# ScalarE's stores on its own DMA queue, bonus and gate loads on GpSimd's, and two PSUM banks counted as taken in a hand-planned TensorE order

## The chip, the cores and the metric

The kernel runs on one core of one Trainium2 chip. TensorE (PE in the profile) does the matrix products, VectorE (DVE), ScalarE (ACT) and GpSimd (POOL) the elementwise work, and SyncE (SP) here only issues DMAs. The metric is device time in microseconds from launch to end. Three runs of the kernel before took 1831.24, 1832.81 and 1837.26 us, a median of 1832.81.

## The reference, cut to what matters

One layer over 1024 prompt tokens and 64 sample tokens (8 sequences of 8), model width 1024, all in float32:

```python
h = rmsnorm(x, norm_g)
q, k, v, ga, ps, gb, ma, mb = split(h @ w_in)
o = sliding-window attention(q, k, v)            # 16 heads, window 128, sinks, bias
ya = (o * silu(ga)) @ w_out_a
z = ps + (shift(ps) - ps) * mu                   # branch B: r, k, v and two low-rank inputs
decay = exp(-exp(-softplus(-(w0 + tanh(wl) @ w2)) - 0.5));  a = sigmoid(a0 + al @ a2)
kk = normalise(k * k_k);  k = k * (1 + (a - 1) * k_a)
for t: S = S * decay + (S @ -kk) (kk * a)^T + v k^T;  y = S @ r     # 16 heads, state 64 x 64
yb = (groupnorm(y) * lnx_g + lnx_b + sum(r * k * r_k) * v) * silu(gb) @ w_out_b
out = x + (sigmoid(ma) * ya + sigmoid(mb) * yb) @ w_o;  y = rmsnorm(out)
```

The results also hold the last 128 keys and values, the last shift rows and the final states.

## The kernel before

Tokens lie along the free dimension, channels on the 128 partitions. A dense product of one 128-column tile of the weights (`mm3`, tile `d`) is split in three passes of high and low parts, 24 matmuls for each of three chunks of 364, 364 and 360 tokens. It lands in one of two PSUM banks with the tag `d`.

The span has three stages. `start` norms the input. `rwkv` runs branch B, the dense products of the projections woven in. `attention` and `final` do branch A and the output.

In `rwkv` the prompt is cut in 16 steps s: four pairs of 128-channel groups by four quarters of 256 tokens (the last quarter has the 64 sample tokens too). A step goes through these streams, each a Python generator:

- `preps`: for each group of the pair, `quarter` loads keys and receptances (`zk`, `zr`), multiplies the low-rank inputs (`lo`, two results) and the squared norms (`kn`), and makes the arrays `Pp`, `kkn` and `KB`; `bonus` makes `sum(r k r_k) v` and stores it in `d_b`. ScalarE's first operation on the next keys, `kkn` (L648), waits for the load of `zk`.
- `fronts`: `scores` makes the key-query products `A` for both groups, 8 small matmuls into two banks; ScalarE (`ab`, L787) and VectorE (`am`, `X`, L793 and L794) copy them out; `invert` sends `ab` through DRAM (L831, L838), solves 15 short triangular steps on VectorE and sends the result back; `turn` transposes values and keys (`t_..v`, `t_..k`).
- `merges` and `chains`: the merge of the inverse (`q_..`) and the recurrence itself, four chunks with the products `c` and `y`.
- `samples` (`sample_chunk`, products `ss_a` to `ss_y`) and `posts` (`post`: group norm, bonus `bt` and gate `gt` loaded from DRAM, three products on GpSimd, store).
- last, the stream of dense products, which fills what the others leave free. `spill` is such a filler: it copies a result out (`copy`), or takes a sigmoid (`sig`) or a SiLU (`silu`), and stores it.

TensorE's order is written out by `drive`, a planner that walks the generators with a clock of its own (`clk`): a step that yields a delay and a bank's tag is ready when the delay is over and the bank's time in `free` has come. The first ready stream of the list above (chains, merges, fronts, preps, samples, posts, dense) goes on. After a step, each tag in `self.used` gets `free = clk + HOLD`, with `HOLD` 2.0. Only `ps` with one buffer puts a tag there. The tag `a` has two buffers, used by `A`, by the second result `lo` and by `kn`; it is not counted in `rwkv`. The first result `lo`, the transposes, `bo` and all of `ss_..` share the one bank `m`.

The other engines' instructions are put in order by a scheduler, from priorities and its own estimates. Each engine works through its order strictly, DMA issues included: an issue that waits holds up whatever stands behind it. In `rwkv` SP issues all loads and stores but those of `zz`, `gz`, `y`, the weights and half of `dinv`, which GpSimd issues. ScalarE issues none.

Of the kernel before, what the change touches and what calls it, by code (L numbers as in the profile page):

```python
# [11 lines left out]
AF = mybir.ActivationFunctionType  # L12
# [69 lines left out]
class Prog:  # L82
# [346 lines left out]
    def spill(self, idx, dst, kind="copy", scale=1.0):  # L429

        nc, ep = self.nc, self.ep

        def evac(c0, c1, ps):
            t = ep.tile([P, 364], F32, tag="zz", name=f"sp{idx}_{c0}", bufs=3)[:, :c1 - c0]
            if kind == "copy":
                nc.scalar.activation(t, ps, AF.Copy, scale=scale)
            else:
                x = ps
                if kind == "silu":
                    x = ep.tile([P, 369], F32, tag="pad", name=f"sx{idx}_{c0}", bufs=3)[:, :c1 - c0]  # L440
                    nc.scalar.activation(x, ps, AF.Copy)
                self.sig_neg(t, t, x, -1.0, 0.0)
                if kind == "silu":
                    nc.gpsimd.tensor_tensor(t, x, t, ALU.mult)
            for d, a, b in dst:
                lo, hi = max(a, c0), min(b, c1)
                if lo < hi:
                    nc.sync.dma_start(d[:, lo - a:hi - a], t[:, lo - c0:hi - c0])
        yield from self.dense(idx, self.hhi, self.hlo, evac)
# [204 lines left out]
    def quarter(self, g, q, gi, f, pre):  # L654
        nc, ep, cp = self.nc, self.ep, self.cp_
        nm = f"{g}_{q}"
        smp = q == 3
        n = 320 if smp else 256
# [5 lines left out]
        w2, zk, kkn, zr = pre  # L664
        yield f"pf{g}_{q}", WD + 4.0 * gi, "m"

        res = []
        pl = [self.ps("m", f"lo{nm}0"), self.ps("a", f"lo{nm}1", 2)]
        for j in range(2):
            t = E("e1", 2)  # L670
            ps = pl[j]
# [93 lines left out]
    def scores(self, g, q, gi, f):  # L765

        nc = self.nc
        nm = f"{g}_{q}"
        S, ab = f["q"][gi], f["ab"]
# [3 lines left out]
        for c0, cn, n0 in sets:  # L773
            mi, ms = (C_SI, C_SS) if c0 else (C_MI, C_MS)
            yield WA if c0 or gi else WR
            pvs = [self.ps("a", f"A{nm}{c0}{h}", 2).rearrange("p (c x) -> p c x", c=4) for h in range(2)]
            for c in range(cn):
                for h, hr in enumerate(halves):
                    self.mm(pvs[h][:, c, :], lhsT=KB[hr, c0 + c, :, :].rearrange("p a s -> p (a s)"),
                            rhs=S["smp"]["ra"][hr].rearrange("p a s -> p (a s)") if c0 else S["X"][hr, c, h::2, :], start=True, stop=True)  # L780
# [41 lines left out]
    def invert(self, nm, ab, n0, nn):  # L822


        nc, ep = self.nc, self.ep
        nb = 8 * nn
        np_ = 2 * nb
        s1 = self.dp.tile([4 * nn, 32, 32], F32, name=f"s1{nm}")
        s2 = self.dp.tile([2, 4, nn, 16, 16], F32, name=f"s2{nm}")
        for g in range(4):  # L830
            nc.sync.dma_start(s1[g * nn:g * nn + nn].rearrange("n j t -> j n t"), ab[32 * g:32 * g + 32, n0:n0 + nn, 32 * (g % 2):32 * (g % 2) + 32])  # L831
        Mf = ep.tile([P, 272], F32, tag="TM", name=f"TM{nm}", bufs=1)
# [7 lines left out]
        if n0:  # L840
# [3 lines left out]
            for s in range(7):  # L844
                w = 7 - s
# [5 lines left out]
        else:  # L851
            for s in range(15):
                w = 15 - s
# [127 lines left out]
    def sample_chunk(self, g, Z):  # L981
        nc, cp = self.nc, self.cp_
# [9 lines left out]
        nc.scalar.activation(sx[:, 0:2], ps, AF.Copy)  # L992
        nc.vector.tensor_copy(sx[:, 2], ps[:, 1])
        yield None, WH, "m"
# [24 lines left out]
        nc.gpsimd.tensor_tensor(sin, sin, Z["pc"].unsqueeze(2).to_broadcast([P, NB, HD]), ALU.mult)  # L1019
        nc.sync.dma_start(self.O["swkv"][g], sin)  # L1020

    def post(self, g, nm, t, w, y):
# [3 lines left out]
        rs = cp.tile([P, 320], F32, tag="gb", name=f"gn{nm}", bufs=2)[:, :w]  # L1026
        nc.sync.dma_start(bt, self.d_b[g][:, t:t + w])
        yield None, WP, "t"
# [12 lines left out]
        gt = cp.tile([P, 320], F32, tag="gb", name=f"gt{nm}", bufs=2)[:, :w]  # L1041
        nc.sync.dma_start(gt, self.d_g[g][:, t:t + w])
        nc.gpsimd.tensor_tensor(y, y, bt, ALU.add)
# [554 lines left out]
```

## Time and profile before

| | |
|---|---|
| median of three runs | 1832.81 us |
| the profiled execution | 1828.53 us |
| its span, first to last instruction | 1826.7 us |
| TensorE busy | 1686.3 us, 92% |
| VectorE, ScalarE, GpSimd busy | 1001.7, 899.5, 647.0 us |
| mean granted TensorE clock | 0.962 |

The page gives each engine's busy time, then the span in 40 slices, then the chain of work that ended last. A busy share says little by itself. What counts is where TensorE stands idle, what ended each such wait, and at what clock it went on.

### The profile page before, as it was taken

To read this page: it belongs to the slowest core of one execution; us is meant where nothing else is said; L and a number is where in the kernel's file an instruction comes from. 1 tells how busy PE (TensorE), PEld (TensorE's weight loads), DVE (VectorE), ACT (ScalarE), POOL (GpSimd) and SP (SyncE) were. 2 spreads that over 40 slices of the span, in tenths; PEclk is the share of its full clock that TensorE was granted. 3 is DMA by queue.
4 is the path that set the end of the run, shared out by engine and by line. 5 is a ranking of instruction groups with operands and counts; after the bars stand their busy time and mean duration, and the time that the engine had idled before them with its cause. 6 is when DMAs were issued, how large, how long until landed. Compare 5 with 4: busy or idle time off the path is not lost.

```text
span 1826.7 us, 36891 instructions
## 1 busy us (share of the span) xinstructions
PE 1686.3 (92%) x13792; PEld 1579.2 (86%) x13792; DVE 1001.7 (55%) x2840; ACT 899.5 (49%) x2257; POOL 647.0 (35%) x902
## 2 busy tenths in 40 slices
PE   6989889888988989889989899999999999999997
PEld 4889789787888878878988888999999999999997
DVE  5322655766766756675445655330566676544533
ACT  6445545544544555455546554535466655422332
POOL 5466445544655553445654233543100000000000
PEclk8899989998999999999999899999999899999999
DMA  4334433343433344432334342323521434464521
GB/s 159 108 123 138 106 100 98 104 105 96 120 90 108 97 122 113 109 93 89 102 119 124 112 105 72 90 86 112 175 67 57 155 109 149 140 204 136 197 80 61
DMA packets 233682, 206.86 MB, mean 113 GB/s; under 512 B 135904, under 2 KB 202608, under 8 KB 233472
## 3 DMA queue, kind: packets, MB, share of 16 engines
q1 hardware_dynamic: 214624, 149.33, 28.6%
q0 software_dynamic: 18880, 55.17, 9.4%
q8 instruction: 109, 1.79, 0.4%
q14 instruction: 69, 0.57, 0.1%
HBM read 140.42 MB, written 65.98 MB: 113 GB/s over the span
## 4 chain that ended last, share of the span: by engine, by line
PE 59%; DVE 16%; DMA 9%; issue 4%; POOL 4%; ACT 3%; SPq 2%; DVEq 0%; POOLq 0%; ACTq 0%
PE d L110 35%; PE wo L110 5%; PE c L110 3%; DVE TR L858 3%; DVE Tt L856 2%; PE s L110 2%; PE o L110 2%; DVE KB L715 2%; PE y L110 2%; PE pt L108 1%; PE A L110 1%; DMA TM<-s 1%; DMA s<-TR 1%; DMA wraw<-in_w 1%; SPq L838 1%
## 5 line engine op out<-in xcount | busy, mean ns | idle before, releaser
L110 PE MATMUL d<-hhi,whi 128*128 128x364 f32 (+1 forms) x1656 | 590.7, 357 | 14.8 <-ACT zz L391 4.3
L110 PE MATMUL d<-hlo,whi 128*128 128x364 f32 (+1 forms) x1656 | 559.7, 338 | 12.2 <-DVE hlo L339 8.3
L110 PEld LDWEIGHTS d<-hhi,whi 128*128 128x128 f32 x1656 | 323.2, 195 | 23.8 <-ACT zz L391 4.9
L110 PEld LDWEIGHTS d<-hlo,whi 128*128 128x128 f32 x1656 | 323.2, 195 | 23.7 <-DVE hlo L339 12.9
L110 PE MATMUL d<-hhi,wlo 128*128 128x364 f32 (+1 forms) x1656 | 339.5, 342 | 0.0
L110 PEld LDWEIGHTS d<-hhi,wlo 128*128 128x128 f32 x1656 | 283.9, 193 | 4.6 <-issue 1.6
L171 POOL TENSOR_TENSOR wlo<-wraw,whi 128x1024 fp32r<-128x1024 f32 x56 | 135.4, 2417 | 82.2 <-ACT whi L170 43.6
L170 ACT ACTIVATE whi<-wraw 128x1024 fp32r<-128x1024 f32 x90 | 94.9, 1054 | 75.7 <-PE d L110 55.9
L1433 POOL TENSOR_TENSOR xr<-xr,frs 128x256 f32<-128x256 f32 x2 | 1.8, 932 | 346.8 <-ACT frs L1430 346.8
L392 POOL TENSOR_TENSOR zz<-zz,pad 128x364 f32<-128x364 f32 (+1 forms) x75 | 72.7, 969 | 58.4 <-ACT zz L391 22.6
L948 POOL TENSOR_TENSOR sp<-vsu,pc 64x128 f32<-64x128 f32 x128 | 54.2, 424 | 97.7 <-DVE vsu L970 88.5
L390 ACT ACTIVATE pad<-d,prm 128x364 f32<-128x364 f32 (+1 forms) x75 | 40.7, 542 | 89.5 <-PE d L110 86.7
L856 DVE TENSOR_TENSOR Tt<-TM,TR 128x30 f32<-128x30 f32 (+10 forms) x240 | 58.6, 244 | 33.6 <-DMA TM<-s 28.3
L1172 ACT ACTIVATE sc<-sc,st 128x256 f32<-128x256 f32 (+1 forms) x128 | 61.8, 485 | 23.7 <-DVE st L1168 23.7
L1083 POOL TENSOR_TENSOR ylo<-ys,yhi 128x364 fp32r<-128x364 f32 (+1 forms) x6 | 6.5, 1084 | 180.8 <-PE ptc L108 153.7
L715 DVE TENSOR_TENSOR KB<-e,sg 64x256 f32<-64x256 f32 x128 | 65.6, 522 | 3.6 <-PE t_10k L108 1.5
L858 DVE TENSOR_TENSOR TR<-TR,Tt 128x30 f32<-128x30 f32 (+10 forms) x240 | 64.1, 267 | 5.9
L877 POOL DMA_DIRECT2D dinv<-s x80 | 42.5, 538 | 68.0 <-DMA s<-TR 68.0
L110 PE MATMUL d<-ol,whi 128*128 128x364 f32 (+1 forms) x192 | 64.2, 334 | 1.4 <-DVE ol L230 1.4
L110 PE MATMUL d<-oh,whi 128*128 128x364 f32 (+1 forms) x192 | 64.0, 334 | 1.4 <-ACT oh L229 1.4
L110 PE MATMUL d<-yhi,whi 128*128 128x364 f32 (+1 forms) x192 | 64.2, 334 | 0.0
L110 PE MATMUL d<-ylo,whi 128*128 128x364 f32 (+1 forms) x192 | 63.6, 331 | 0.0
(348 smaller groups left out, 3743.1 us busy)
## 6 DMA issues: line engine op xcount, KB each, us to landing
wraw<-in_w POOLq DMA_DIRECT2D x56, 512.0 KB, 4.0
wraw<-in_w SPq DMA_DIRECT2D x37, 512.0 KB
d_z<-zz POOLq DMA_DIRECT2D x48, 182.0 KB, 2.3
zv<-d_z SPq DMA_DIRECT2D x48, 128.0 KB
w<-d_c SPq DMA_DIRECT2D x24, 256.0 KB
d_m<-sp SPq DMA_DIRECT2D x32, 182.0 KB
stageo<-d_o SPq DMA_DIRECT2D x8, 544.0 KB
d_z<-zz POOLq DMA_DIRECT2D x24, 180.0 KB, 4.1
```

The lines of the kernel that those rows point to most:

```text
L108: self.nc.tensor.transpose(out, lhsT, rhs)
L110: self.nc.tensor.matmul(out, lhsT=lhsT, rhs=rhs, **kw)
L170: nc.scalar.activation(hi, raw, AF.Copy)
L171: (nc.vector if self.dve_lo else nc.gpsimd).tensor_tensor(lo, raw, hi.bitcast(F32), ALU.subtract)
L390: nc.scalar.activation(pad[:, 1:1 + m], ps[:, :m], AF.Copy, scale=mu)
L392: nc.gpsimd.tensor_tensor(z[:, :m], z[:, :m], pad[:, 0:m], ALU.add)
L715: nc.vector.tensor_tensor(KB[hr, :4, j, :], self.v64(t)[hr], self.d64(Pi, 1)[hr], ALU.mult)
L856: nc.vector.tensor_tensor(tv, M[:np_, s:s + 1, s + 1:16].to_broadcast([np_, cc, w]), R[:np_, 0:cc, s:s + 1].to_broadcast([np_, cc, w]), AL ...
L858: nc.vector.tensor_tensor(R[:np_, 0:cc, s + 1:16], R[:np_, 0:cc, s + 1:16], tv, ALU.add)
L877: (nc.gpsimd if a else nc.sync).dma_start(D[o:o + 16, n0:n0 + nn, 16 * a:16 * a + 16], s2[a, g].rearrange("n j t -> j n t"))
L948: nc.gpsimd.tensor_tensor(sp[h], vsu[h, c, :, h], pc[h, c].unsqueeze(2).to_broadcast([64, 2, HD]), ALU.mult)
L1172: nc.scalar.activation(sc[k], sc[k], AF.Exp, bias=st[:, 0, k:k + 1], accum_out=st[:, 1, k:k + 1])
```

## The change

Six edits:

1. `spill` stores its tiles from ScalarE's DMA queue, and those of kind `silu` from GpSimd's, in place of SP's.
2. `scores` puts `a` in `self.used`, so the planner holds the tag for 2.0 after the products `A`.
3. `quarter` yields once more after its wait for `m`, until `a` is free, and only then issues `lo` and `kn`.
4. `invert` issues its four stores of `ab` from ScalarE's queue (those of the samples stay on SP's).
5. `sample_chunk` makes the third part of `sx` on ScalarE, not VectorE, and stores the sample state from GpSimd's queue.
6. `post` loads `bt` and `gt` from GpSimd's queue.

```diff
@@ spill
-                    nc.sync.dma_start(d[:, lo - a:hi - a], t[:, lo - c0:hi - c0])
+                    (nc.gpsimd if kind == "silu" else nc.scalar).dma_start(d[:, lo - a:hi - a], t[:, lo - c0:hi - c0])
@@ quarter
         yield f"pf{g}_{q}", WD + 4.0 * gi, "m"
+        yield None, 0.0, "a"
@@ scores
             pvs = [self.ps("a", f"A{nm}{c0}{h}", 2).rearrange("p (c x) -> p c x", c=4) for h in range(2)]
+            self.used.add("a")
@@ invert
-            nc.sync.dma_start(s1[g * nn:g * nn + nn].rearrange("n j t -> j n t"), ab[32 * g:32 * g + 32, n0:n0 + nn, 32 * (g % 2):32 * (g % 2) + 32])
+            (nc.sync if n0 else nc.scalar).dma_start(s1[g * nn:g * nn + nn].rearrange("n j t -> j n t"), ab[32 * g:32 * g + 32, n0:n0 + nn, 32 * (g % 2):32 * (g % 2) + 32])
@@ sample_chunk
         nc.scalar.activation(sx[:, 0:2], ps, AF.Copy)
-        nc.vector.tensor_copy(sx[:, 2], ps[:, 1])
+        nc.scalar.activation(sx[:, 2], ps[:, 1], AF.Copy)
...
-        nc.sync.dma_start(self.O["swkv"][g], sin)
+        nc.gpsimd.dma_start(self.O["swkv"][g], sin)
@@ post
-        nc.sync.dma_start(bt, self.d_b[g][:, t:t + w])
+        nc.gpsimd.dma_start(bt, self.d_b[g][:, t:t + w])
...
-        nc.sync.dma_start(gt, self.d_g[g][:, t:t + w])
+        nc.gpsimd.dma_start(gt, self.d_g[g][:, t:t + w])
```

How the orders move is seen at one step of the recurrence, third quarter of the second pair. In the names below `A_100` and `A_101` are the two banks of key-query products, `lo_20` and `lo_21` the two low-rank products of the next quarter, `kn` its norms. TensorE before:

```order
L110 MATMUL A_100_5330<-X_739,KB_1_4852 128x128
L110 MATMUL A_101_5331<-X_739,KB_1_4852 128x128
L110 MATMUL lo_20_5347<-zl_2_5215,w_2_2_5217 128x256 x2
L110 MATMUL lo_21_5348<-zl_2_5215,w_2_2_5217 128x256 x2
L110 MATMUL kn_2_5359<-kkn_2_5221,bc 128x256
L110 MATMUL d_1_5172<-hhi_149,wlo_4823 128x364 x4
L110 MATMUL q_0c<-du_0_5328,ab_0_4537 32x32 x16
L110 MATMUL d_2_5419<-hhi_154,whi_4822 128x360
L110 MATMUL d_2_5419<-hlo_155,whi_4822 128x360
...
L110 MATMUL A_100_5424<-X_740,KB_1_4959 128x128
```

Behind the change, the same place on TensorE:

```order
L110 MATMUL A_100_5318<-X_739,KB_1_4837 128x128
L110 MATMUL A_101_5319<-X_739,KB_1_4837 128x128
L110 MATMUL ss_a<-ras_3_3635,sin_5159 64x2x8 x16
L110 MATMUL q_0c<-du_0_5316,ab_0_4525 32x32 x16
L110 MATMUL d_1_5272<-hhi_149,whi_4875 128x364
L110 MATMUL d_1_5272<-hlo_150,whi_4875 128x364
...
L110 MATMUL lo_20_5382<-zl_2_5198,w_2_2_5200 128x256 x2
L110 MATMUL lo_21_5383<-zl_2_5198,w_2_2_5200 128x256 x2
L110 MATMUL kn_2_5394<-kkn_2_5204,bc 128x256
L110 MATMUL A_100_5396<-X_740,KB_1_4955 128x128
```

Four dense matmuls, a round of the merge and the first sample product now stand between the first group's `A` and `lo`. The second group's `A`, which had four dense matmuls, a merge round and four more between `kn` and itself, now follows `kn` at once.

ScalarE at that place before (`e` is made from `lo`, `sg` from `e`):

```order
L648 ACTIVATE kkn_2_5365<-zk_2_5363,prm 128x256
L787 ACTIVATE ab_1_5198<-A_100_5330 64x256
L674 ACTIVATE e_2_2_5349<-lo_20_5347,prd 128x256
L675 ACTIVATE e_2_2_5349<-e_2_2_5349 128x256
L787 ACTIVATE ab_1_5198<-A_101_5331 64x256
...
L787 ACTIVATE ab_1_5198<-A_100_5424 64x256
L920 ACTIVATE ti<-q_0d 32x8x32 x2
L815 ACTIVATE vsu_1_5199<-t_10v 64x4x64 x2
L787 ACTIVATE ab_1_5198<-A_101_5425 64x256
```

And now (line numbers are one or two higher):

```order
L789 ACTIVATE ab_1_5181<-A_100_5318 64x256
L994 ACTIVATE sx_5352<-ss_a 128x128
L995 ACTIVATE sx_5352<-ss_a 128x64
L789 ACTIVATE ab_1_5181<-A_101_5319 64x256
L675 ACTIVATE e_2_2_5384<-lo_20_5382,prd 128x256
...
L789 ACTIVATE ab_1_5181<-A_100_5396 64x256
L833 DMA s_10_5413<-ab_1_5181 32x8x32
L922 ACTIVATE ti<-q_0d 32x8x32 x2
L833 DMA s_10_5413<-ab_1_5181 32x8x32
L817 ACTIVATE vsu_1_5182<-t_10v 64x4x64 x2
L789 ACTIVATE ab_1_5181<-A_101_5397 64x256
L833 DMA s_10_5413<-ab_1_5181 32x8x32 x2
```

Both copies of the first group's `A` now stand ahead of `e`, `kkn` of the next load has left this place, and four DMA issues stand among the copies of the second group's `A`.

GpSimd in a `post` of the first step, the second group, before:

```order
L1040 TENSOR_TENSOR ysb_01_2554<-ysb_01_2554,gn_0_3331 128x256
L1043 TENSOR_TENSOR ysb_01_2554<-ysb_01_2554,bt_0_3330 128x256
L948 TENSOR_TENSOR sp_13_3527<-vsu_1_2133,pc_1_2134 64x128 x2
L877 DMA dinv<-s_20_3208 16x8x16 x4
L1044 TENSOR_TENSOR ysb_01_2554<-ysb_01_2554,gt_0_3510 128x256
```

And now:

```order
L1042 TENSOR_TENSOR ysb_01_2554<-ysb_01_2554,gn_0_3323 128x256
L169 DMA wraw_3710<-in_w 128x1024
L1044 DMA gt_0_3502<-d_g_108 128x256
L1045 TENSOR_TENSOR ysb_01_2554<-ysb_01_2554,bt_0_3322 128x256
L1029 DMA bt_1_3662<-d_b_115 128x256
L424 TENSOR_TENSOR gz_0_3538<-gx_0_3539,gz_0_3538 128x364
L425 DMA d_g_110<-gz_0_3538 128x364
L1046 TENSOR_TENSOR ysb_01_2554<-ysb_01_2554,gt_0_3502 128x256
```

GpSimd now issues the gate's load itself, behind a load of weights, and waits for it a few instructions later.

TensorE's order is the same in both kernels up to the first `lo` that comes behind an `A`, and over its last 2206 rows, from within the attention stage to the end.

## Rows read from the trace of the kernel before

**Rows 1.** The page: busy time of engines (us, share of the span, instructions), and the granted clock of TensorE in 40 slices.

```profile
PE 1686.3 (92%) x13792; PEld 1579.2 (86%) x13792; DVE 1001.7 (55%) x2840; ACT 899.5 (49%) x2257; POOL 647.0 (35%) x902
PEclk8899989998999999999999899999999899999999
```

**Rows 2.** Busy time by stretch (`start` with the first projections, `rwkv`, and the rest): us, busy time of each engine with its instructions, then granted clock, DMA share and GB/s.

```profile
0.00:125.00 125.00, 97.00 (x456) 84.78 (x457) 42.59 (x77) 58.56 (x129) 66.25 (x92) 0.86 0.38 132
125.00:1250.00 1125.00, 1028.06 (x9559) 959.55 (x9558) 646.69 (x1879) 577.04 (x1486) 554.95 (x784) 0.97 0.38 104
1250.00:1827.00 577.00, 561.25 (x3781) 534.84 (x3779) 312.40 (x885) 263.89 (x644) 25.83 (x28) 0.98 0.40 128
```

**Rows 3.** What TensorE waited for over the span, by line: us in total, times, longest.

```profile
PE lo L110 <- ACT ab L787: 26.8, 13, 4.4
PE c L110 <- DVE vsu L960: 11.4, 12, 2.9
PE c L110 <- DVE xs L955: 9.9, 6, 3.9
PE ss_b L110 <- DVE sx L993: 8.6, 3, 3.8
...
PE ss_b L110 <- DVE sg L686: 2.8, 1, 2.8
...
PE A L110 <- ACT ab L787: 0.6, 1, 0.6
```

**Rows 4.** The timeline from 348.7 to 354 us, TensorE, ScalarE and VectorE at one place where `lo` follows `A`: start, us, engine, line, operation, count, and in brackets the idle time before it and what ended it.

```profile
348.71 0.33 PE L110 MATMUL d<-hhi,whi 128*128 128x364 f32 x1
348.88 0.33 PE L110 MATMUL d<-hlo,whi 128*128 128x364 f32 x1
...
349.82 1.16 PE L110 MATMUL A<-X,KB 64*128 64x128 f32 x16
...
352.45 0.43 DVE L794 TENSOR_TENSOR X<-A,rco 64x256 f32<-64x256 f32 x1
...
352.81 0.38 ACT L787 ACTIVATE ab<-A 64x256 f32<-64x256 f32 x1
...
353.24 0.79 PE L110 MATMUL lo<-zl,w 128*128 128x256 f32 x2 [1.83 <-ACT ab L787]
```

**Rows 5.** The timeline of ScalarE from 669 to 672 us and the TensorE row that waits for it.

```profile
669.50 0.51 ACT L648 ACTIVATE kkn<-zk,prm 128x256 f32<-128x256 f32 x1 [2.12 <-DMA zk<-d_z]
...
671.66 0.38 ACT L787 ACTIVATE ab<-A 64x256 f32<-64x256 f32 x1
...
672.09 0.80 PE L110 MATMUL lo<-zl,w 128*128 128x256 f32 x2 [4.20 <-ACT ab L787]
```

**Rows 6.** The timeline at one place where `A` comes after `kn`: ScalarE's and VectorE's copies out of the two banks between them.

```profile
302.77 0.70 PE L110 MATMUL kn<-kkn,bc 128*128 128x320 f32 x2
...
302.97 0.53 ACT L674 ACTIVATE e<-lo,prd 128x320 f32<-128x320 f32 x1
...
303.81 0.49 DVE L696 TENSOR_SCALAR kkn<-kn 128x320 f32<-128x320 f32 x1
```

**Rows 7.** The timeline at one sample step: the two parts of `sx`, and the product that reads them.

```profile
748.20 0.25 ACT L992 ACTIVATE sx<-ss_a 128x128 f32<-128x128 f32 x1
...
753.08 0.22 DVE L993 COPY sx<-ss_a 128x64 f32<-128x64 f32 x1
...
753.36 0.80 PE L110 MATMUL ss_b<-con,sx 128*128 128x128 f32 x2 [3.77 <-DVE sx L993]
```

**Rows 8.** Busy time in the seven stretches at half clock that come right behind a wait of `lo` (four) or of `ss_b` (three); columns as in the second group. The first of each kind, and the sum of all seven.

```profile
353.23:356.64 3.41, 3.40 (x71) 2.69 (x72) 2.52 (x5) 2.91 (x9) 1.18 (x2) 0.50 0.48 190
...
506.83:513.66 6.83, 6.20 (x24) 6.21 (x25) 1.00 (x5) 2.43 (x6) 4.73 (x9) 0.50 0.24 67
...
sum 34.13, PE 30.83 PEld 28.07 DVE 13.41 ACT 15.93 POOL 12.10; mean PE 4.40 PEld 4.01 DVE 1.92 ACT 2.27 POOL 1.73
```

**Rows 9.** Two lines' own views: how long SP takes for one DMA issue (ns, least, median, most).

```profile
L831 SPq DMA_DIRECT2D s<-ab x80: 302/418/1788, 190.6 to 1142.9; - x80
...
L448 SPq DMA_DIRECT2D d_m<-sp x48: 319/357/587, 555.7 to 1183.6; - x48
```

**Rows 10.** What SP's queue waited for over the span: us in total, times, longest.

```profile
SPq L448 <- ACT sp L222: 83.9, 23, 10.1
...
SPq L831 <- ACT ab L787: 74.9, 27, 12.9
...
SPq L646 <- DMA d_b<-zk: 35.0, 19, 3.8
```

**Rows 11.** Groups of GpSimd's instructions: count, busy us, mean ns, idle time before them and what ended it.

```profile
L1044 POOL TENSOR_TENSOR ysb<-ysb,gt 128x256 f32<-128x256 f32 (+1 forms) x32 | 26.4, 824 | 38.0 <-DMA gt<-d_g 37.5
...
L1045 POOL DMA_DIRECT2D d_y<-ysb x32 | 19.0, 594 | 12.8 <-POOL ysb L1044 6.5 <-issue 6.0 <-DVE TR L858 0.3
```

**Rows 12.** What ScalarE and VectorE waited for over the span: us in total, times, longest.

```profile
ACT kkn L648 <- DMA zk<-d_z: 72.8, 22, 10.8
...
DVE pad L387 <- POOL zz L392: 27.3, 5, 13.5
```

## The prediction

> **What bounds the kernel now.** I read the page's busy times first, then the busy times by stretch, then TensorE's waits, then the places themselves. TensorE is busy 92% of the span [rows 1]. In `rwkv`, from 125 to 1250 us, it is busy 1028 of 1125 us, so some 97 us stand idle there; the stretch behind it has 16 idle us in 577 [rows 2]. When the recurrence ends, dense work is still left, so time that TensorE loses in `rwkv` is lost for good. The change reaches `rwkv` almost alone, and the sum is made there.
>
> The waits name one culprit: `lo` on `ab`, 26.8 us in 13 waits [rows 3]. One place shows why [rows 4]. `A` ends at 350.98. Its banks are free only when VectorE's last `X` (352.88) and ScalarE's second `ab` (353.19) are done, 2.2 us later, but the order lets `lo`, which needs one of them, follow at once. TensorE stands 1.83 us. Another shows a long one [rows 5]: ScalarE sits 2.12 us on a load (`kkn`), the second `ab` ends at 672.04, and `lo` has waited 4.20 us. The `ss_b` waits are of the same kind: VectorE copies the third part of `sx` at 753.08, 4.6 us after ScalarE's part was done at 748.45, because it stands behind other work in its order [rows 7]. These two lines give 8.6 + 2.8 = 11.4 us [rows 3].
>
> Such a wait is paid twice. In the seven stretches at 0.50 behind waits of `lo` and `ss_b`, 34.13 us long, TensorE is busy 30.83 us at the lower of its two levels, 1.2 GHz, where 2.4 would have done the work in half: 15.4 us [rows 8].
>
> **The change part by part**, against the span of 1826.7 us (the whole execution took 1828.5, 4.3 under the median of the runs, and I add the same difference to the median).
>
> *The wait of `lo`.* In the planned order `lo` came at once, or within 0.9 us, behind `A` at 14 places. Counting the matmuls between at the trace's pitch (0.17 us for a dense one, 348.71 to 348.88 [rows 4]), there are now 1.2 to 2.6 us between. The second `lo`, the one that needs the bank, starts 0.3 us after the first, so a usual evacuation of 2.2 us leaves 0 to 0.7. The order of ScalarE helps: at most of these places both `ab` now stand ahead of the sigmoids of `lo`, and `kkn` has left several. The three waits over 3 us should keep about half. I leave 7 of 26.8: **-20** (ends -14, if only the 1.2 us of filling counts at each, and -27).
>
> *What follows it.* `lo` and `kn` take the same two banks, and these the planner still does not count. At most of the 14 places the second `A` now follows `kn` at once or after one short product, where some eight dense matmuls were. At one place of today `kn` ends at 303.47 and VectorE has its bank free at 304.30, 0.83 later; ScalarE's read of the second `lo` ends at 303.50 [rows 6]. So a new wait of about 0.5 us at each of 14 places: **+7** (2 to 14, the upper end if ScalarE is 1 us late, as it is behind one weight split or copy).
>
> *The bank `m`.* The new wait for `a` comes after the one for `m`, so another stream may take `m` in between, and does at five places: `ss_a` four times, a key transpose once, with 0 to 0.9 us between it and `lo`. ScalarE frees `m` with two copies of 0.25 each, behind one `ab` of 0.38 [rows 4, 7]; at the transpose two DMA issues stand ahead too. **+4** (1 to 9).
>
> *`sx` on ScalarE.* Its first part is read there anyway, 0.25 us; the second follows at once. **-9** of the 11.4 (0, if ScalarE is as late as VectorE was, to -11).
>
> *The clock.* Of 15.4 us I take 11 back, and give 3 to new waits long enough to bring the clock down: **-8** (0 to -15).
>
> *ScalarE's issues.* 64 stores of `ab` and 72 of filler results in `rwkv`. The trace shows no issue on ScalarE; the nearest rows are SP's, 0.36 to 0.42 us each [rows 9], so some 50 us on an engine that is busy 577 of 1125 [rows 2]. Two of them stand ahead of the copy of the value transpose at 16 places, 0.84 us before TensorE's key transpose needs the bank; the plan has 2 us there, which hides most. **+3** (0, if all is covered, to +13 if none is).
>
> *GpSimd's issues.* 64 loads, 8 state stores and 9 filler stores, 81 at 0.594 us, GpSimd's own price [rows 11], are 48 us on an engine busy 555 of 1125 [rows 2]. TensorE never waits for GpSimd directly there. What it can hold up is `zz`, for whose buffers VectorE waits [rows 12], and the state products. The wait for the gate's load exists already, 37.5 us [rows 11]; GpSimd now issues that load itself, right after the product that frees its buffer. **+3** (-2 to +40).
>
> *SP's queue.* It loses 222 issues and the waits ahead of them: it stood 83.9 us for filler results and 74.9 for `ab` [rows 10], with loads behind. ScalarE's 72.8 us of waiting for `zk` [rows 12] can shrink, but those loads wait for the bonus store that frees their buffer too (35.0 us [rows 10]). **-2** (0 to -6). The Trainium skill, page "DMA: Bandwidth & Descriptors", section "Issuing engines are not separate DMA queues", speaks against any gain here: issuing from several engines saves only the sequencer's time to start a DMA. By that this term is 0 and the time 2 us more; the rows above speak for waiting in line as a second thing that is saved.
>
> Sum: -20 + 7 + 4 - 9 - 8 + 3 + 3 - 2 = **-22 us**. 1832.8 - 22 = **1811 us**.
>
> **The rivals.**
>
> *All of it comes off.* ScalarE's new order takes the evacuations out of the way; -27 for `lo`, -11 for `ss_b`, -13 for the clock, new waits 2 + 1, and the issues +3 and +3 with -2: -44, 1789 us. For it: the long waits are ScalarE's order, and that order has changed. Against it: the second `A` right behind `kn`.
>
> *The wait only moves*, so that the change doesn't do what it says: `a` is counted for `A` alone, and the waits of `lo` turn up at the second `A` (+14) and at `m` (+9), with ScalarE's issues at +13 and new drops of the clock that use up what the old ones give back: -20 - 9 + 14 + 9 + 13 - 2 is -5, some 1828 to 1834 us, no change. For it: 14 places with next to nothing between `kn` and `A`. Against it: by the row of VectorE's copy that wait is a third of the old one [rows 6].
>
> *GpSimd becomes late*, slower. At each of the 32 posts it issues the gate's load and soon stops for it; with 0.594 for the issue and its landing behind, often with a load of weights just ahead in the same queue, `zz` and the state products come later, VectorE stands at L387 (already 27.3 us, once 13.5 [rows 12]), and the recurrence behind it. If 1.25 us of each post reach TensorE, that is +40 in place of +3: -22 + 37 = +15, 1848 us. It turns the result once 0.8 us of a post arrive (25 us over 32). For it: GpSimd works in strict order. Against it: half its time is free, and it waits for the same load today. The Trainium skill, page "DMA: Bandwidth & Descriptors", section "Latency and other measured facts", puts the first byte of a GpSimd DMA at about 1 us against 0.6 on the other queues; by that the 32 gate loads come 13 us later in all, an estimate from that page alone. No run here shows it.
>
> **How the numbers follow.** The sum 0.52 (its own range 1797 to 1826); all of it 0.12; only moved 0.19; GpSimd late 0.17. The range of 80% leaves out most of the second and the upper two thirds of the last: **1795 to 1840**. About 0.3% either way, 5.5 us, is what a measurement of this kernel can tell from no change. Under 1827.3 lie nearly all of the first two and a third of the third: **faster 0.68**, same 0.15, slower 0.17.
>
> **What would show it.** Right: `lo` on `ab` under 10 us, `ss_b` on `sx` under 3, the seven stretches at half clock mostly gone, `rwkv` idle near 75 us, and the tail from attention on unchanged. The steps of my additions: `A` waiting for `e` (L675) or `kkn` (L697) by 5 to 10 us, `lo` waiting for `sx` or `kbt` by about 4. Wrong: VectorE's waits for GpSimd's `zz` twice as long, with `c` on `vsu` and `xs` well over their 21 us; or the clock under 0.962 with the idle time moved, not gone.

## The result, and the profile after

| | before | after |
|---|---|---|
| median of four runs | 1832.03 us | 1853.03 us |
| ratio, 95% interval | | 1.0109 [1.0084, 1.0134] |
| profiled span | 1826.7 us | 1852.3 us |

The change makes the kernel 1.1% slower; the prediction had it 1.2% faster. The page of the changed kernel, its busy times and granted clock (against [rows 1]):

```profile
PE 1696.3 (92%) x13792; PEld 1591.6 (86%) x13792; DVE 1014.1 (55%) x2832; ACT 897.0 (48%) x2265; POOL 694.3 (37%) x983
PEclk8899999989899989999989999999999999999999
```

Busy time by stretch (against [rows 2]; us, then PE, PEld, DVE, ACT, POOL, clock, DMA share, GB/s):

```profile
125.00:1250.00 1125.00, 1010.33 (x9344) 944.67 (x9343) 654.76 (x1860) 559.14 (x1460) 579.98 (x838) 0.95 0.37 101
1250.00:1852.30 602.30, 587.64 (x3998) 561.00 (x3996) 316.95 (x896) 279.47 (x678) 48.28 (x55) 0.99 0.40 127
```

TensorE is busy 10 us longer with the same 13792 matmuls, at a mean granted clock of 0.956 against 0.962, and stands idle 15.6 us longer. GpSimd has 47 us more, for 81 DMA issues more. TensorE's waits over the span (against [rows 3]):

```profile
PE c L110 <- DVE vsu L962: 29.9, 16, 8.0
PE c L110 <- DVE xs L957: 20.0, 8, 6.3
PE bo L110 <- DVE vss L1007: 9.2, 3, 3.8
PE ss_a L110 <- DMA sin<-in_wkv: 8.9, 4, 3.9
...
PE ss_d L110 <- DVE ve L1015: 6.8, 2, 5.4
...
PE lo L110 <- ACT sx L995: 4.7, 1, 4.7
...
PE A L110 <- ACT e L675: 1.8, 3, 0.9
...
PE A L110 <- DVE kkn L697: 1.6, 3, 0.5
```

The wait of `lo` for `ab` is gone, and that of `ss_b` for `sx` too. `A` waits for `e` and `kkn` as foretold, but only 3.4 us. The recurrence's `c`, 21.3 us in [rows 3], now waits 49.9 us for VectorE. The stretches of `rwkv` at the lower clock, the first one and the sum of all 25 (against [rows 8], which held seven of 16):

```profile
224.13:230.96 6.83, 6.01 (x28) 5.38 (x29) 1.56 (x5) 4.05 (x12) 6.51 (x9) 0.50 0.35 83
...
sum 119.44, PE 103.51 PEld 97.57 DVE 60.23 ACT 38.69 POOL 46.70; mean PE 4.14 PEld 3.90 DVE 2.41 ACT 1.55 POOL 1.87
```

and the same sum over the 16 such stretches of the kernel before:

```profile
sum 78.49, PE 66.55 PEld 59.65 DVE 32.14 ACT 29.53 POOL 27.53; mean PE 4.16 PEld 3.73 DVE 2.01 ACT 1.85 POOL 1.72
```

TensorE works 103.5 us at 0.50 (1.2 GHz) in place of 66.6; at 2.4 GHz half would do, so 18.5 us more are lost in `rwkv`. Not all of that stays: behind 1250 us the clock is 0.99, where it was 0.98 before, and over the whole span the busy time grows by 10 us. These are also single executions, and the clock differs from one to the next: 0.956 to 0.963, mean 0.960, in four of the changed kernel; 0.954 to 0.973, mean 0.963, in 91 of the kernel before. So the size of the loss is uncertain. The gain of 8 that the prediction gave the clock shows nowhere.

GpSimd's loads (line groups; idle time before them at the end; against [rows 11]):

```profile
L1046 POOL TENSOR_TENSOR ysb<-ysb,gt 128x256 f32<-128x256 f32 (+1 forms) x32 | 26.6, 832 | 28.7 <-DMA gt<-d_g 28.4
...
L1044 POOL DMA_DIRECT2D gt<-d_g x32 | 18.6, 580 | 10.4 <-POOL ysb L1042 7.4 <-issue 3.0
L1029 POOL DMA_DIRECT2D bt<-d_b x32 | 17.8, 555 | 7.1 <-POOL ysb L1045 6.8 <-DMA d_b<-zk 0.3
```

### The profile page after: what moved, and what is told of

The parts are those of the page before. It is cut to its first block, busy times and chain, and to the rows that moved or that the text cites. A ratio compares the mean times of both kernels' runs of the same rounds, so it can differ in the third digit from the quotient of the medians.

```text
span 1852.3 us, 36813 instructions
## 1 busy us (share of the span) xinstructions
PE 1696.3 (92%) x13792; PEld 1591.6 (86%) x13792; DVE 1014.1 (55%) x2832; ACT 897.0 (48%) x2265; POOL 694.3 (37%) x983
## 3 DMA queue, kind: packets, MB, share of 16 engines
q0 software_dynamic: 23168, 67.86, 11.5%
## 4 chain that ended last, share of the span: by engine, by line
PE 57%; DVE 18%; DMA 8%; issue 5%; POOL 4%; ACT 3%; SPq 2%; DVEq 0%; ACTq 0%; POOLq 0%
PE d L110 35%; PE wo L110 5%; DVE Tt L858 3%; PE c L110 3%; DVE TR L860 3%; DVE KB L716 2%; PE s L110 2%; PE y L110 2%; PE o L110 2%; PE A L110 2%; PE pt L108 1%; DMA TM<-s 1%; SPq L840 1%; DMA wraw<-in_w 1%; POOL wlo L171 1%
## 5 line engine op out<-in xcount | busy, mean ns | idle before, releaser
L110 PE MATMUL d<-hhi,whi 128*128 128x364 f32 (+1 forms) x1656 | 588.6, 356 | 15.6 <-ACT zz L391 5.0
L110 PE MATMUL d<-hhi,wlo 128*128 128x364 f32 (+1 forms) x1656 | 346.9, 347 | 0.0
L110 PEld LDWEIGHTS d<-hhi,wlo 128*128 128x128 f32 x1656 | 289.2, 197 | 4.8 <-issue 0.7
L858 DVE TENSOR_TENSOR Tt<-TM,TR 128x30 f32<-128x30 f32 (+10 forms) x240 | 75.2, 313 | 16.5 <-DMA TM<-s 10.5
L110 PE MATMUL c<-vsu,kbt 128*128 128x128 f32 x256 | 43.3, 294 | 30.0 <-DVE vsu L962 29.9
L110 PEld LDWEIGHTS c<-vsu,kbt 128*128 128x128 f32 x256 | 38.0, 200 | 37.4 <-DVE vsu L962 35.2
```

The source lines that it names most:

```text
L110: self.nc.tensor.matmul(out, lhsT=lhsT, rhs=rhs, **kw)
L858: nc.vector.tensor_tensor(tv, M[:np_, s:s + 1, s + 1:16].to_broadcast([np_, cc, w]), R[:np_, 0:cc, s:s + 1].to_broadcast([np_, cc, w]), AL ...
```

## The experiments

Each of e1 to e18 was timed in five rounds beside the kernel before on one chip, but not all on the same chip, so ratios to the kernel before are compared, not times. `After` is the changed kernel, with the ratio of the four runs above; `before` is the one before.

| kernel | ratio | 95% |
|---|---|---|
| after | 1.0109 | 1.0084 to 1.0134 |
| e1: after, `bt` and `gt` back on SP | 1.0033 | 1.0013 to 1.0052 |
| e2: after, state store back on SP | 1.0117 | 1.0086 to 1.0148 |
| e3: before, banks alone (edits 2, 3) | 0.9997 | 0.9974 to 1.0019 |
| e4: after without the banks | 1.0075 | 1.0048 to 1.0102 |
| e5: e3, all uses counted | 0.9916 | 0.9885 to 0.9948 |
| e6: after, bias of `bt` made earlier | 1.0108 | 1.0080 to 1.0136 |
| e7: e3, the same | 1.0054 | 1.0030 to 1.0077 |
| e8: before, the same | 0.9994 | 0.9975 to 1.0014 |
| e9: after, all `dinv` loads on SP | 1.0174 | 1.0144 to 1.0204 |
| e10: after, `gt` back on SP | 1.0083 | 1.0052 to 1.0114 |
| e11: after, `bt` back on SP | 1.0131 | 1.0105 to 1.0156 |
| e12: after, all uses counted | 1.0024 | 1.0007 to 1.0040 |
| e13: e1 with 64 idle loads on GpSimd | 1.0186 | 1.0163 to 1.0210 |
| e14: before, `bt` and `gt` on GpSimd | 1.0117 | 1.0084 to 1.0150 |
| e15: before, stores on ScalarE | 1.0038 | 1.0018 to 1.0058 |
| e16: e5 with `sx` on ScalarE | 0.9923 | 0.9899 to 0.9948 |
| e17: e1 with 64 small stores on GpSimd | 1.0862 | 1.0828 to 1.0895 |
| e18: the same stores on SP | 1.0706 | 1.0672 to 1.0740 |

TensorE's order is the changed one in e1, e2, e3, e6, e7, e9 to e11, e13, e17 and e18, and that of before in e4, e8, e14 and e15, so orders and queues are told apart. Where the idle time lies, from the profiled runs: gaps of TensorE over 50 ns from 125 us to the recurrence's end, by the product that waited, and the time lost at the lower clock there (half of the work done at it), in us. Each row is one execution, and the last column is the least sure:

| | idle | lo | c | ss | A | rest | clock |
|---|---|---|---|---|---|---|---|
| before | 96.9 | 30.7 | 27.9 | 15.3 | 0.8 | 22.2 | 33.3 |
| after | 114.6 | 6.4 | 51.5 | 18.2 | 4.3 | 34.2 | 51.8 |
| e1 posts back | 102.9 | 6.6 | 43.1 | 16.3 | 4.3 | 32.6 | 36.6 |
| e3 banks alone | 95.9 | 7.1 | 41.1 | 14.7 | 7.5 | 25.5 | 38.9 |
| e4 no banks | 104.0 | 27.1 | 42.8 | 11.7 | 2.0 | 20.5 | 44.0 |
| e5 all counted | 84.9 | 2.8 | 30.6 | 29.4 | 4.5 | 17.6 | 33.1 |
| e14 posts alone | 108.4 | 31.4 | 32.5 | 17.7 | 0.8 | 26.0 | 44.8 |
| e15 stores alone | 103.7 | 23.6 | 38.2 | 19.3 | 1.3 | 21.3 | 44.6 |

**Which edit costs.** e1 and e2 undo one move of a queue, e3 does the banks alone, e4 leaves the banks out.

```diff
 e1  -        nc.gpsimd.dma_start(bt, ...)
     +        nc.sync.dma_start(bt, ...)          # gt likewise
 e2  -        nc.gpsimd.dma_start(self.O["swkv"][g], sin)
     +        nc.sync.dma_start(self.O["swkv"][g], sin)
 e3  +        yield None, 0.0, "a"                # on the kernel before
     +            self.used.add("a")
 e4  the two lines of e3 taken out of the changed kernel
```

> The changed kernel with the loads of bt and gt back on SP's queue, all else kept; TensorE's order is the same. Theory Loads (GpSimd issues the bonus and gate loads late, ScalarE stands for them, and the recurrence behind it): near the sum that I forecast, 1810 to 1828 us, ScalarE's wait for bt falls from 73 us to 40 or less, and the waits of c from 51 to under 35. Theory Order (the new order on TensorE leaves the recurrence too little time wherever the loads are issued): 1843 to 1855 us, c still waits 45 us or more. Theory State (the sample state's store on GpSimd holds up SP): 1845 to 1855.

> The changed kernel with the store of the sample state back on SP's queue, all else kept. Theory State: SP's wait at the load of the next state falls from 53 us to 10 or less, the waits of ss_a for that load (8.9 us) go, and the time falls to 1815 to 1835 us. Theories Loads and Order: only the 8.9 us and what they cost at half clock go, 1838 to 1852 us.

> The kernel before with the bank count alone (the tag a put in use by scores, and quarter's second yield): TensorE's order of the changed kernel, all DMAs and sx where they were. Theory Loads and theory State: the waits of lo fall from 27 us to under 10 and little comes in their place, 1812 to 1826 us. Theory Order: the waits of c rise as in the changed kernel, to 45 us or more, and the time is 1840 us or more.

> The changed kernel without the bank count: TensorE's order of the kernel before, with the new queues and sx on ScalarE. Theory Loads: the waits of lo are back and those of c are over 40 us, 1850 us or more. Theory State: much the same, 1845 or more, with SP's long wait at the load of the state. Theory Order: 1815 to 1832 us, the waits of c at 20 to 30 us as before.

The loads of `bt` and `gt` cost 1.0109 - 1.0033 = 0.76%, 14 us; the state store nothing that can be told (1.0117), so "State" falls. The banks, the heart of the forecast gain, bring nothing. What is left between e1 and e3 is 0.36%. No theory had the whole: e1 (1834 us) lies between the ranges of "Loads" and "Order", e4 (1840) between those of "Order" and "State", and e3 (1826) is far under the 1840 of "Order".

**Why the banks bring nothing.** e5 counts the bank `a` wherever it is used, and asks for `m` again once `a` is free; e16 adds the edit of `sx`.

```diff
 e5  (on e3)
             yield f"pf{g}_{q}", WD + 4.0 * gi, "m"
             yield None, 0.0, "a"
     +       yield None, 0.0, "m"
     ...
             pk = self.ps("a", f"kn{nm}", 2)
     +       self.used.add("a")
     ...
     -            yield WA if c0 or gi else WR
     +            yield None, WA if c0 or gi else WR, "a"
 e16 (on e5)
     -        nc.vector.tensor_copy(sx[:, 2], ps[:, 1])
     +        nc.scalar.activation(sx[:, 2], ps[:, 1], AF.Copy)
```

> The kernel before with the bank count made whole: quarter waits for m again after a, kn takes the tag a too, and scores waits for a before its products. TensorE's order differs from that of the banks-only kernel. Theory Ate-itself (the unguarded second A and the bank m ate the gain of the banks): the waits of A, lo and t (19.6 us in the banks-only kernel) fall under 8 us, c stays near 41, and the time falls by 8 to 15 us, to 0.992 to 0.996 of the kernel before. Theory Late-recurrence (TensorE only arrives earlier, and VectorE and ScalarE are not ready): those waits fall too, but c and q rise by as much, and the time is within 0.3% of the kernel before.

> The kernel with banks counted throughout (0.9916), with the third part of sx made on ScalarE as in the change. Its samples' products wait 29 us, of which some 19 stand behind VectorE's other work at ss_d, ss_y and ss_a. The prediction's step: ss_b no longer waits for VectorE's copy, worth up to 9 us where that wait exists; in this order it is small, so a theory 'No wait left' expects no change, ratio 0.990 to 0.993, some 1815 us; theory 'Still a gain' expects the 5 us of VectorE's time freed and the clock with it, ratio under 0.989, some 1809 us.

Dense matmuls that stand between the products of the two banks, counted in the traces:

| | A to lo: none between | kn to A: none between |
|---|---|---|
| before | 12 of 29 | 0 of 30 (least 4) |
| after (and e3) | 0 of 28 (least 4) | 13 of 29 |
| e5 | 0 of 21 (least 4) | 0 of 22 (least 8) |

The half count moves the bare place from `lo` to `A`. One such place after the change, TensorE, ScalarE and VectorE in the timeline (start, us, engine, line, operation, idle time before):

```profile
186.72 0.59 PE L110 MATMUL kn<-kkn,bc 128*128 128x256 f32 x2
...
187.35 0.42 DVE L697 TENSOR_SCALAR kkn<-kn 128x256 f32<-128x256 f32 x1 [1.65 <-PE kn L110]
187.35 0.84 ACT L675 ACTIVATE e<-lo,prd 128x256 f32<-128x256 f32 x2
...
188.25 0.94 PE L110 MATMUL A<-X,KB 64*128 64x128 f32 x12 [0.93 <-ACT e L675]
```

This costs little by itself (A 7.5 us in e3). But idle time in `rwkv` is 95.9 us in e3 against 96.9: what `lo` gives, `c` (+13.2), `A` (+6.7) and the merge and transposes take. With all uses counted, 12 us of idle go, `c` is back near 30, and the kernel is 0.8% faster than before. "Ate-itself" has the time, a little past its range, but not all of the way there: it had `c` stay near 41, and the waits of `A`, `lo` and the transposes fell from 19.6 to 11.4 us, not under 8, while the samples' products wait 29.4 us in place of 14.7. That the count was half done, and that the full one wins, is shown; which of its three lines wins is not told apart, and that `c` waits longer because dense work which had stood ahead of it now stands ahead of `lo` is argued only: with the stores alone, on the old order, `c` rises by 10 us too (e15). `sx` gains nothing here, as "No wait left" had it.

**What the loads on GpSimd cost by.** The first theory was ScalarE's stand for `bt`, 73.4 us in the change. e6 to e8 take ScalarE's operation on `bt` out of `post` and add the same bias ahead of the store of the bonus.

```diff
     -        nc.scalar.activation(bt, bt, AF.Identity, bias=self.par(Q_LB + g))
 bonus:
     +        nc.scalar.activation(zk[:, :n], zk[:, :n], AF.Identity, bias=self.par(Q_LB + g))
              nc.sync.dma_start(self.d_b[g][:, a0:a0 + n], zk[:, :n])
```

> The changed kernel, with the addition of the group norm's bias to bt moved from post (where ScalarE waits for the load of bt) to bonus, so that ScalarE has no instruction that waits for that load; GpSimd still issues it. TensorE's order is the same. Theory Loads (ScalarE standing for bt holds up gn, then VectorE's copy of ysb, then c): ScalarE's 73 us of waiting for bt go, VectorE's wait for gn falls from 67 us to under 40, c from 51 to under 40, and the ratio to the kernel before falls from 1.011 to 1.003 or less. Theory Issue (GpSimd's time for issues is what costs): c stays over 45 and the ratio at 1.008 to 1.012.

> The bank count alone, with the same move of the bias; loads on SP. ScalarE waits 65 us for bt in the banks-only kernel. Theory Loads: the gain of the banks shows once that wait is gone, 0.985 to 0.993 of the kernel before. Theory Late-recurrence (other causes): 0.996 to 1.002.

> Control: the kernel before with the move of the bias alone; ScalarE waits 40 us for bt there. Theory Loads: 0.993 to 0.999. Theory Late-recurrence: 0.998 to 1.003.

Nothing is won (1.0108 against 1.0109). That alone doesn't refute the theory, because ScalarE's new operation in `bonus` stands as long for VectorE's product. What speaks against it is e1: with 14 us won back, ScalarE stands for `bt` almost as long as in the change. The change, e1 and e6:

```profile
ACT bt L1035 <- DMA bt<-d_b: 73.4, 22, 6.7
...
ACT bt L1035 <- DMA bt<-d_b: 69.4, 21, 10.5
...
ACT zk L731 <- DVE zk L730: 72.7, 17, 7.5
```

On the banks alone the same move costs 0.57% (e7 against e3), which neither theory had and nothing here explains; on the kernel before it does nothing (e8).

TensorE's order being the same, the change and e1 can be laid side by side, matmul by matmul: by 1247 us the change is 24.7 us behind (16.1 at the end of the span), and some 21 of them arise in the seven stretches of 25 us that end at 338, 388, 489, 820, 971, 1046 and 1247. The one at 464 to 489, GpSimd, VectorE and TensorE:

```profile
462.50 0.58 POOL L1044 DMA_DIRECT2D gt<-d_g  x1 [2.98 <-issue]
...
464.15 0.55 POOL L1029 DMA_DIRECT2D bt<-d_b  x1 [0.31 <-DMA d_b<-zk]
...
464.72 2.12 POOL L879 DMA_DIRECT2D dinv<-s  x4
...
468.39 0.45 DVE L882 STREAM_TRANSPOSE dt<-dinv 128x256 f32<-128x256 f32 x1 [5.92 <-DMA dinv<-s]
468.56 2.33 POOL L171 TENSOR_TENSOR wlo<-wraw,whi 128x1024 fp32r<-128x1024 f32 x1
468.76 2.40 DVE L746 SCALAR_TENSOR_TENSOR X<-kkn,Pp 64x256 f32<-64x256 f32 x1
...
472.60 0.61 DVE L962 COPY vsu<-c 64x128 f32<-64x128 f32 x2
...
473.27 1.01 PE L110 MATMUL c<-vsu,kbt 128*128 128x128 f32 x3 [7.96 <-DVE vsu L962]
```

Behind the two loads stand GpSimd's four loads of the inverse's result; SP had issued its half by 461.0. VectorE stands 5.92 us for them, with the copy that the recurrence needs behind. Three runs vary this.

```diff
 e9  -   (nc.gpsimd if a else nc.sync).dma_start(D[o:o + 16, ...], s2[a, g]...)
     +   nc.sync.dma_start(D[o:o + 16, ...], s2[a, g]...)
 e10 -   nc.gpsimd.dma_start(gt, ...)
     +   nc.sync.dma_start(gt, ...)
 e11 -   nc.gpsimd.dma_start(bt, ...)
     +   nc.sync.dma_start(bt, ...)
```

> The changed kernel, with all loads of the inverse's result (dinv) issued from SP; half of them stood on GpSimd's queue in both kernels. Three theories of the 0.76% that the loads of bt and gt cost on GpSimd. Theory 'Behind': GpSimd stops at a load of gt or bt (for the bonus store or a buffer), and the dinv loads behind it go out late: at 466.8 against 461.0 on SP, and at 843.0 against 838.7, after which VectorE stands for dinv 5.92 and 3.1 us and the recurrence behind it; it expects 8 to 11 us less than the changed kernel, some 1842 us, ratio 1.005, and those two waits under 2 us. Theory 'Gate': what costs is that the product with the gate ends later, so that the buffer of the next post's group norm comes late and VectorE stands at the copy of the centred values (41.6 us against 30.8 with the loads on SP); it expects under 4 us here, some 1850 us, ratio 1.010. Theory 'Issue': what costs is GpSimd's time, 0.57 us an issue; 64 issues go from it here, as many as the loads were, so it expects most of the 14 us back, some 1840, and GpSimd's own products earlier everywhere.

> The changed kernel with the gate's loads (gt) back on SP and the bonus loads (bt) still on GpSimd. Theory 'Gate': nearly all of the 14 us come back, some 1837 us, ratio 1.004, VectorE's wait at the copy of the centred values back near 31 us. Theory 'Behind': half or less, since GpSimd still stops for the bonus store ahead of dinv, 3 to 7 us, some 1845 us. Theory 'Issue': half, 7 us, some 1844 us, and the next kernel gives the other half.

> The changed kernel with the bonus loads (bt) back on SP and the gate's loads (gt) still on GpSimd. Theory 'Gate': at most 3 us, some 1849 us, ratio 1.010, VectorE's wait at the copy of the centred values still near 40 us. Theory 'Behind': 4 to 8 us, since the stop for the bonus store ahead of dinv is gone, some 1845 us. Theory 'Issue': half, 7 us, some 1844 us.

In e9 that place is cured (`c` waits 3.54 us at 468.95), and VectorE's wait for `dinv` falls from 38.3 to 24.0 us, but the kernel is no faster (1.0174), with 80 issues more on SP and VectorE standing 12.7 us for a load (`TR`) that SP issues: "Behind" is true of the place and false of the sum. "Issue" falls short too, since it expected 1.005 here. e10 and e11 can't be told from the change. Against e1 the bonus loads alone cost 0.50% (e10) and the gate's loads alone 0.98% (e11), where both cost 0.76%: each move costs by itself, and the two don't add. "Gate" expected 1.004 of e10, "Behind" and "Issue" some 1.007 of e11, so none of the three has the whole.

e14 makes the same move on the kernel before, so that nothing else is in play.

> The kernel before, with the loads of bt and gt issued from GpSimd and nothing else changed. If this edit costs by itself what it costs inside the change, the ratio is 1.0076, some 1844 us. Theory 'Only together': the loads cost because the new order of TensorE has the recurrence waiting (41 us in place of 28 with the banks' edit alone), so that a late VectorE always shows; on the old order, whose idle time lies at lo, they cost under 0.3%, ratio under 1.003, some 1833 us.

It costs 1.17% alone. "Only together" falls. Its profiled execution shows no one waiter: idle rises by 11.5 us, spread over `c`, `bo`, `ss` and `lo`, and the clock takes another 11.5. The next three ask whether the issues themselves cost, or what they wait for.

```diff
 e13 (on e1)  in each post, behind each of the two loads
     +        nc.gpsimd.dma_start(cp.tile([P, 1], F32, tag="du", ..., bufs=8), self.I["par"][:, 0:1])
 e17 (on e1)  behind the product with rs and behind the sum with bt
     +        du = cp.tile([P, 1], F32, tag="du", ..., bufs=8)
     +        nc.gpsimd.tensor_copy(du, y[:, 0:1])
     +        nc.gpsimd.dma_start(self.dp.tile([P, 1], F32, ...), du)
 e18 as e17, but
     +        nc.sync.dma_start(self.dp.tile([P, 1], F32, ...), du)
```

> The changed kernel with the loads of bt and gt back on SP (1.0033 by itself), and two more loads in each post issued from GpSimd, at the same places: a column of parameters, 128 rows of one number, into a small tile that nothing reads. They wait for no other engine's work. Theory 'Issue': 64 issues at 0.57 us of GpSimd's time are the cost; the ratio is back near 1.010, some 1846 us. Theory 'Wait': what costs is that GpSimd stops in its order for the bonus store and the gate's buffer, and that the gate's load goes out only after GpSimd's own earlier product; then the ratio stays under 1.006, some 1835 us.

> The changed kernel with the loads of bt and gt back on SP (1.0033), and in each post two small stores more from GpSimd: a copy of one column of y into a small tile, behind the product with the group norm and behind the sum with the bonus, and a store of that tile to a scratch place in DRAM. They stand in GpSimd's order where the moved loads stood, and wait for GpSimd itself alone. Theory 'Issue': 64 issues at 0.55 us (and 64 small copies) on GpSimd, ahead of its products, are what costs: ratio 1.009 to 1.013, some 1848 us. Theory 'Wait': the loads cost because of what they wait for and because they go out late; these issues do neither: ratio under 1.006, some 1837 us. In between both have a share.

> The control: the same copies on GpSimd, but the 64 small stores issued from SP. What this kernel costs over 1.0033 is the copies, the transfers and SP's queue; only what the one before costs over this one is GpSimd's issuing. Theory 'Issue': 1.003 to 1.006, some 1836 us, and 0.4% or more under the one before. Theory 'Wait': both the same within 0.3%.

e13 didn't test what it was for: with nothing to wait for, the loads were all put at 83 to 118 us, as the line's own view shows (ns least, median, most; first and last start):

```profile
L1030 POOL DMA_DIRECT2D dubt<-in_par x32: 537/537/605, 82.6 to 117.2; - x32
```

There GpSimd's load of the next weights stands behind them and goes out at 124.22 us, and TensorE stands for the split of those weights:

```profile
PE d L110 <- ACT whi L170: 37.8, 1, 37.8
```

At 130 us this kernel is 32 us behind e1, and it stays so to the end. 64 issues of 0.54 us are 35 us: where nothing covers GpSimd, almost all arrives.

In e17 and e18 the small stores themselves cost over 6%, from either engine, so the theories' numbers don't apply; what tells is the difference. It is 1.56%, 29 us, for the same 64 stores issued from GpSimd and not SP. Lines of e17, then of e18:

```profile
L1045 POOL DMA_DIRECT2D ddg<-dug x32: 540/587/628, 310.8 to 1426.6; - x32
...
DMA to landing us min/median/max: 7.2/8.2/10.0
```

```profile
L1045 SPq DMA_DIRECT2D ddg<-dug x32: 319/376/1553, 311.4 to 1391.9; - x32
```

That speaks for "Issue", 0.45 us of each 0.59 arriving at the end, where e9 speaks against it. It is no clean price: GpSimd's own `dinv` loads stand in line with the slow stores in e17, and VectorE's copy `dt` waits 104.6 us for `dinv` there, 82.1 in e18.

**The rest of the queues.**

```diff
 e15 (on before)
     -    nc.sync.dma_start(d[:, lo - a:hi - a], ...)
     +    (nc.gpsimd if kind == "silu" else nc.scalar).dma_start(d[:, lo - a:hi - a], ...)
     -    nc.sync.dma_start(s1[...], ...)
     +    (nc.sync if n0 else nc.scalar).dma_start(s1[...], ...)
 e12 (on after) the lines that e5 adds to e3
```

> The kernel before, with the stores of filler results and of ab issued from ScalarE (those of kind silu from GpSimd) and nothing else changed. Theory 'Stores cost': they are the remaining 0.36% between the kernel with banks alone and the change without the posts' loads, since ScalarE issues in its order 0.33 to 0.45 us each between copies that TensorE waits for: ratio 1.003 to 1.007. Theory 'Stores free': SP's freed queue pays for them, as the prediction had it (+3 and -2 us): ratio 0.998 to 1.002, and the remaining 0.36% is the state store or sx.

> The changed kernel with the banks counted throughout: quarter asks for the bank m again after a, the norms kn put a in the planner's count too, and the products A wait for it. On the kernel before, this guard took the banks' edit from 0.9997 to 0.9916, 0.8%. Theory 'Apart': the losses of the queues lie in the recurrence's and samples' waits, which the guard doesn't touch, so the two add up: 1.011 - 0.008, ratio 1.003, some 1837 us. Theory 'Together': with the products of the banks spread, the dense work that covered a late engine is used up elsewhere, so that the guard is worth half or less behind the queues' edits: ratio 1.007 or more, some 1845 us. Theory 'Queues need it': both tie up on the same waits, and the guarded change is faster than the kernel before, ratio under 0.998.

The stores cost 0.38%, which is what was left between e1 and e3. ScalarE issues them at SP's price:

```profile
L448 ACTq DMA_DIRECT2D d_m<-sp x48: 326/327/406, 557.0 to 1200.2; - x48
...
L831 ACTq DMA_DIRECT2D s<-ab x64: 309/358/1786, 190.4 to 1152.7; - x64
```

e12 is 1.0024 - 0.9916 = 1.08% over e5, and the change 1.12% over e3: the queues cost on the good order what they cost on the poor one. "Apart" is right. On the order of the kernel before they don't add up so: loads (e14) and stores (e15) cost 1.17 and 0.38% alone, and all queue edits with `sx` on ScalarE only 0.75% (e4). The wait of `ss_b` is 11.4 us before, 16.2 in e15 and 1.6 in e4, so a gain of `sx` can be the difference; no run has `sx` alone on that order. e5 is the fastest kernel, with e16 level: the banks counted throughout, and every queue left where it was.

## Why the prediction was wrong

The sum was -22 us; about +20 was measured. In the changed order of TensorE the parts make that up: banks 0 (e3, within 4 us), loads of the posts +14 (e1 against the change), and the 7 us between e3 and e1, which are the price of the stores alone (e15). Two steps failed. The first is the gain of the banks, with `sx` and the clock hung on it: -26 in the sum, nothing measured. The second is the price of the issues, on GpSimd +3 in place of +14 and on ScalarE and SP +1 in place of +7.

1. **"I leave 7 of 26.8: -20"** was right as a wait: all waits of `lo` fell from 30.7 to 6.4 us. So were "+7" (3.4 to 7) and "+4" (5.7, `sx` 4.7 and `kbt` 1.0). The failed step is the sum of these three: it treated a wait removed as time won. No term asked what is late next when TensorE reaches the recurrence earlier. `c` was, by 13 us, and the whole edit came to nothing. The rival "the wait only moves" had this outcome for the banks, but named `A` and `m` as its places, not `c`. Its sum is also added up wrongly: its terms make +5, not -5, so 1838 us.
2. **`sx`, -9**, was counted twice. In e3 no wait of `ss_b` for `sx` is left, though VectorE still makes it there: the new order alone removes that wait. What remains is a wait of `lo` for `sx`, 5.3 us in e3 and 4.7 in the change, so the edit had next to nothing left to win. e16 gives 0 on the full count. On the old order, where the wait exists, it stays untested alone.
3. **The clock, -8**: no such gain. In the profiled executions 16 stretches at 1.2 GHz in `rwkv` became 25, 18.5 us more lost there and 10 us over the span. The term gave 3 us to new waits, but as many long waits came as went: TensorE's waits of over 2 us up to the recurrence's end were 17 and are 20. The sign for being wrong, a clock under 0.962 with the idle time moved, is what came.
4. **GpSimd's issues, +3 (-2 to +40)**: measured +14 inside the change and +21 alone. The bound held; the value was taken at the end near "half its time is free". Half an engine's time free says nothing while others wait for its next result. "It waits for the same load today" is true, and that wait even fell (37.5 to 28.4 us), while the cost came.
5. **ScalarE's issues +3 and SP's queue -2**: together +1 was forecast, +7 measured (3 to 11 by the interval), and no run tells the two apart. The Trainium skill, page "DMA: Bandwidth & Descriptors", section "Issuing engines are not separate DMA queues", gives no gain beyond the sequencer's time; that agrees with a total in which no gain from SP's shorter queue shows.
6. **The rival "GpSimd becomes late"**, 1848 us, came nearest to 1853, in part by luck, since it kept the -25 of the other terms. Its route was wrong: VectorE's wait at L387 stayed (26.6 against 27.3 us in [rows 12]), and so did the other one for `zz`, at L396 (30.7 against 28.4). Its price, 1.25 us of each post, was too high: 14 to 21 us over 32 posts are 0.4 to 0.7. The Trainium skill's rule beside it (page "DMA: Bandwidth & Descriptors", section "Latency and other measured facts", a later first byte on GpSimd's DMAs) now has rows that agree in direction: the gate's load lands 3.3 us after its issue from GpSimd in the change and 2.8 in e14 (medians), and 2.1 from SP in e5.

What stays open: through which waits the 14 us of the loads reach TensorE. One place of seven is shown, either load costs alone, and the rest is spread over many short waits and the clock. Open too are why `c` comes late once `lo` doesn't, and what the move of the bias costs on the banks alone.

## What to carry to other kernels

A plan that counts a shared buffer for one of its users can move the wait to the next user: here the half count won nothing and the full count 0.8%. Before two edits are each given a gain, check that the first doesn't already remove the wait that the second is for. Before moving DMA issues to an engine that "has time", list what stands behind them in its strict order: the posts' 64 loads on GpSimd, at 0.55 to 0.58 us an issue, cost 14 to 21 us. Don't book a gain of the clock for waits removed before it is known what waits in their place.

## What the runs showed of the hardware

**VectorE stands still while GpSimd computes.** At 468.56 above GpSimd splits weights for 2.33 us, and VectorE's operation at 468.76 takes 2.40 us; the same line takes 0.42 at 461.61. So with the inverse's short steps, here in the change (ns least, median, most):

```profile
L860 DVE TENSOR_TENSOR TR<-TR,Tt x240: 153/184/2397, 203.4 to 1178.4; 128x30 f32<-128x30 f32 x24, 128x14 f32<-128x14 f32 x16, 128x24 f32<-128x24 f32 x16, 128x15 f32<-128x15 f32 x8
```

The Trainium skill, page "SBUF — State Buffer", section "Who interferes with whom", says that a VectorE instruction with two inputs in SBUF contends with a GpSimd instruction that reads SBUF, and calls the ports that they share an exclusive lock. The rows agree: VectorE's 2.40 us end 0.27 us behind GpSimd's 2.33. It is in both kernels, and no term of the prediction had it.

**A small store is slow.** 128 rows of 4 bytes take 8.2 us to land in DRAM from GpSimd's queue (median, e17, above); a load of the same shape took 1.9 us (e13). Two such stores per post, with the small copies ahead of them, cost 6.7% of the time from SP and 8.3% from GpSimd over e1.
